# Layer 0's feed-forward, up half: seven block products for eight, weight sums made by accumulating DMAs, and adaLN units spread over single weight units

## The chip, the cores and the metric

One core of a Trainium2 chip runs the kernel. The metric is the device time in microseconds (us) of one execution. The engines named below are PE (TensorE, the matrix products), DVE (VectorE), ACT (ScalarE), POOL (GpSimd) and SP (SyncE, which here does nothing but issue DMAs; POOL issues some too). L97 is line 97 of the kernel's code.

## The reference

Two layers over 512 latent tokens ("x") and 256 context tokens ("c") of width 1024. Layer 0 mixes tokens by retention, layer 1 by differential attention; each layer ends with a gated feed-forward, and scales, shifts and gates of every sub-layer come from a conditioning vector (adaLN). The change is in the feed-forward of layer 0, where latent and context tokens go through the same weights:

```
def conv_ffn(u, w_up, conv_w, conv_b, w_down):
    val, gate = jnp.split(u @ w_up, 2, axis=-1)          # w_up: 1024 x 5632, hidden 2816 = 22 x 128
    return (jax.nn.silu(dwconv3(gate, conv_w, conv_b)) * val) @ w_down
...
    shm, scm, gm, shf, scf, gf = ada_mod(c, ada_w[l], ada_b[l])   # silu(c) @ ada_w + ada_b
    fx = conv_ffn(modulate(rms_norm(h_x, norm_g[l, 2]), shf, scf), ffn_w_up[l], ...)
    fc = conv_ffn(modulate(rms_norm(h_c, norm_g[l, 2]), cshf, cscf), ffn_w_up[l], ...)
```

Everything is float32.

## The kernel before

Every float32 product is made of three products of numbers of fewer bits: `split` writes an operand as H (a rounded copy, by ACT) and L (the rest, operand minus H, by DVE), and `mm3` (L96 to L99) issues H*H, H*L and L*H into the same PSUM bank. Weights come in units of 128 x 1024 (512 KB): SP loads one into `wraw` (three buffers, L64), ACT and DVE split it into `wH` and `wL` (L59, L60).

The stages follow one another: retention of layer 0 (four heads), its output product `ret_out` (`sublayer_out`, banks `pso`, first the latent tokens, then the context), the feed-forward's up half (banks `psf`), its down half (`sublayer_out` again, `pso`), then layer 1. No table sets the order. A scheduler places the instructions in the order of the code, weight loads and splits are pulled ahead by a priority, and a tile pool's number of buffers decides how far ahead a load can run.

The up half works on one block f of 128 hidden columns after another, 22 in all. For each f there are two units, gate and value (class `FFNUp`). Each is 8 row blocks of the weights (k) x 3 products, once over the 512 latent columns `ux` and once over the 256 context columns `uc`: 96 matmuls for one f, 48 of 512 columns and 48 of 256. `conv` then makes the hidden row block: ACT scales the gate (L322), two DVE operations add the neighbours (L323, L325), ACT applies SiLU (L327), and DVE multiplies by the value (L328) into `hTx` and `hTc`, which stay in SBUF until the down half splits them (`lxH`, `lxL`).

Between units `ada_next` computes adaLN values that later sub-layers need: an adaLN unit is one more 512 KB load through the same three `wraw` buffers and one or two DVE reductions (L164). Before the change 36 of the 80 stand in the retention (`ada_next(2)` or `(3)` after groups of weight units) and 44 in the up half, two for each f.

Just ahead of the up half the last steps of `ret_out` are: finish the latent tokens (`fin`, `sc`), transpose and modulate them into `ux` while PE does the context's output product, then the same for the context (`ctx_part`, L854 of the changed code), which runs while PE does the first products over x.

Of the kernel before, what the change touches and what calls it, by code (L numbers as in the profile page):

```python
# [9 lines left out]
F32 = mybir.dt.float32  # L10
# [20 lines left out]
def tile_hybrid_backbone(ctx: ExitStack, tc: tile.TileContext, A, out, dbg=None):  # L31
# [163 lines left out]
    class UT:  # L195
        def __init__(self):
            self.xH = [s2(F32R, name="uxH") for _ in range(KT)]
            self.xL = [s2(F32R, name="uxL") for _ in range(KT)]
            self.cH = self.cL = None

        def add_ctx(self):
            self.cH = [s2(F32R, (P, 2, 256), name="ucH") for _ in range(4)]
            self.cL = [s2(F32R, (P, 2, 256), name="ucL") for _ in range(4)]

        def part(self, p, k):

            if p == "c":
                return self.cH[k // 2][:, k % 2, :], self.cL[k // 2][:, k % 2, :]
            if isinstance(p, int) and p >= 4:
                o = slice((p - 4) * P, (p - 3) * P)  # L210
                return self.cH[k // 2][:, k % 2, o], self.cL[k // 2][:, k % 2, o]
            o = slice(p * P, (p + 1) * P) if isinstance(p, int) else {
                "x": slice(0, 512), "g0": slice(0, 256), "g1": slice(256, 512)}[p]
            return self.xH[k][:, o], self.xL[k][:, o]
# [146 lines left out]

    l0 = tc.tile_pool(name="l0", bufs=1)
# [32 lines left out]
    def ada_w(k):  # L395
        for kh in range(2):
            wada[k, kh] = W(A["ada0"][k * 2 + kh], late=k % 2 == 1, eng=nc.gpsimd if 2 * k + kh in (5, 9, 13, 4, 6, 0) else None, big=True)
# [69 lines left out]
    def first_ctx():  # L467
        U.add_ctx()
        norm_pair(psp, U, "c", xs[4:6], 0, 0)
# [8 lines left out]
    cb = l0p.tile([P, 2, 1024], F32, name="cb")  # L478
# [90 lines left out]
    for h in range(4):  # L569
# [3 lines left out]
        for qi in range(2):  # L573
            px = [bank("psqx") for _ in range(2)]
            pc = bank("psqc", (P, 2, 256))
            for c in range(2):
                w = qw.pop(0) if qw else W(win[w0 + 4 + 2 * qi + c])
                feat(U, w, px[c], "x")
                if h == 0 and qi == 0 and c == 0:
                    first_ctx()  # L580
                    qw.append(W(win[5]))
                    constants()
                    first_gate_ctx()
                feat(U, w, pc[:, c, :], "c")
# [18 lines left out]
            ada_next(2)  # L603
# [72 lines left out]
        ada_next(3)  # L676
# [25 lines left out]
        ada_next(2)  # L702
# [15 lines left out]
    def sublayer_out(nk, unit, lx, lc, chunk, prev, dst_x, dst_c, layer, sub_i, hook, pre):  # L718
# [8 lines left out]
        for k in range(nk - 2):  # L727
            w, lt = W(unit(k)), lx(k)
# [12 lines left out]
        def ahead(k):  # L741
            for j in range(min(k + 3, nk - 1) + 1):
                if j not in lcs:
                    lcs[j] = lc(j)
                if j == len(wcs) and j <= k + 2:
                    wcs.append(W(unit(j), "s6" if j % 2 == 0 else False))
# [5 lines left out]
        u = UT()  # L752
        side = []
# [13 lines left out]
        def keep(t):  # L767
# [3 lines left out]
                4: lambda: (keep(2), sc(2)), 5: lambda: (keep(3), sc(3), tr(0)), 8: lambda: tr(1)}  # L771
# [18 lines left out]
        def ctx_part():  # L790
# [3 lines left out]
            u.add_ctx()  # L794
            norm_pair(psp, u, "c", [xn[4], xn[5]], layer, sub_i)
# [3 lines left out]
    up0 = {}  # L799

    def pre_up():
        return [W(A["up"][0, i], True) for i in range(2)]

    u, ctx_part, first = sublayer_out(
        16, lambda k: A["ret_out"][k], lhs_x(load_y(0, 512)), lhs_c(load_y(512, 768)), 2, tok_src,
        lambda t: rows(h1d, t), lambda t: rows(h1d, t), 0, 1, lambda: y_out(3, prev_y), pre_up)
    flush_rows(psp)
    F = FFNUp(psp, u, 0, True, ada_next)
    F.w[0, 0], F.w[0, 1] = first
    F.run(0, 0, "x")  # L810
    F.run(0, 1, "x")
    ctx_part()
    F.run(1, 0, "x")
    F.conv(0, "x")
    F.run(0, 0, "c")
    F.run(0, 1, "c")
    F.run(1, 0, "c")
    F.conv(0, "c")
    for p in ("x", "c"):
        F.run(1, 1, p)  # L820
    F.conv(1, "x")
    F.conv(1, "c")
    F.rest(2)
# [3 lines left out]
    def pre_in():  # L827
# [3 lines left out]
        NF, lambda k: A["down"][0, k], lhs_x(lambda k: F.hx[k]), lhs_c(lambda k: F.hc[k]), 5, lambda t: rows(h1d, t),  # L831
        lambda t: rows(h2d, t), None, 1, 0, lambda: flush_rows(psp), pre_in)
# [10 lines left out]
    l0.__exit__(None, None, None)  # L843
# [477 lines left out]
    keep = [(k, W(A["down"][1, k], True), lx(k)) for k in range(NF - late, NF)]  # L1321
# [100 lines left out]
```

## Time and profile before

| | before |
|---|---|
| time, median of 3 runs | 2208.4 us (2206.65 to 2209.94) |
| the profiled execution's own time | 2208.85 us |
| its span in the trace | 2207.0 us |
| mean granted PE clock | 0.986 of full speed |
| busy share of the span: PE, DVE, ACT, POOL | 97%, 56%, 38%, 11% |
| up half of layer 0 on PE | 880.68 us to 1249.48 us |

The span is what the trace covers; the time lies 1.85 us above it. The busy shares are means over stages with different limits, so the rows further down take the stages apart by stretches of 40 us. The up half is found by the names of PE's banks: it begins with the first `psf` product and ends with the first `pso` product of the down half.

### The profile page before, as it was taken

To read this page: it belongs to the slowest core of one execution; us is meant where nothing else is said; L and a number is where in the kernel's file an instruction comes from. 1 tells how busy PE (TensorE), PEld (TensorE's weight loads), DVE (VectorE), ACT (ScalarE), POOL (GpSimd) and SP (SyncE) were. 2 spreads that over 40 slices of the span, in tenths; PEclk is the share of its full clock that TensorE was granted. 3 is DMA by queue.
4 is the path that set the end of the run, shared out by engine and by line. 5 is a ranking of instruction groups with operands and counts; after the bars stand their busy time and mean duration, and the time that the engine had idled before them with its cause. 6 is when DMAs were issued, how large, how long until landed. Compare 5 with 4: busy or idle time off the path is not lost. (4 is left out here: it accounts for less than half of the span.)

```text
span 2207.0 us, 28221 instructions
## 1 busy us (share of the span) xinstructions
PE 2150.1 (97%) x11136; PEld 1834.2 (83%) x11136; DVE 1227.3 (56%) x1928; ACT 849.1 (38%) x1494; POOL 243.1 (11%) x310
## 2 busy tenths in 40 slices
PE   7999999999999999999999999999999789999998
PEld 6888888888888888888888888888888678888887
DVE  6656553553553348665445625767797686444524
ACT  5432233332332346322222324654455465333412
POOL 3001101100200101000000001021232151000000
PEclk8999999999999999999999999999999899999999
DMA  7232322322223366434444435611111332333333
GB/s 261 87 111 86 129 78 69 118 92 69 101 86 110 113 212 205 141 117 140 125 128 126 151 105 194 207 51 46 44 44 32 112 122 101 102 97 99 109 97 124
DMA packets 82732, 250.68 MB, mean 114 GB/s; under 512 B 10104, under 2 KB 13480, under 8 KB 82472
## 3 DMA queue, kind: packets, MB, share of 16 engines
q1 hardware_dynamic: 79880, 241.00, 34.0%
q0 software_dynamic: 2720, 7.89, 0.9%
q8 instruction: 87, 1.43, 0.3%
q14 instruction: 45, 0.37, 0.1%
HBM read 232.05 MB, written 16.80 MB: 113 GB/s over the span
## 5 line engine op out<-in xcount | busy, mean ns | idle before, releaser
L60 DVE TENSOR_TENSOR wL<-wraw,wH 128x1024 fp32r<-128x1024 f32 x233 | 286.1, 1228 | 504.9 <-ACT wH L59 503.3
L59 ACT ACTIVATE wH<-wraw 128x1024 fp32r<-128x1024 f32 x259 | 273.9, 1058 | 642.9 <-PE psa L99 182.9
L97 PE MATMUL psf<-uxH,wH 128*128 128x512 f32 (+1 forms) x672 | 258.7, 385 | 0.0
L98 PE MATMUL psf<-uxL,wH 128*128 128x512 f32 (+1 forms) x672 | 258.5, 385 | 0.0
L99 PE MATMUL psf<-uxH,wL 128*128 128x512 f32 (+1 forms) x672 | 258.1, 384 | 0.1
L97 PE MATMUL pso<-wH,lxH 128*128 128x512 f32 x432 | 168.3, 390 | 0.6 <-ACT grow L183 0.3
L98 PE MATMUL pso<-wL,lxH 128*128 128x512 f32 x432 | 168.1, 389 | 0.0
L99 PE MATMUL pso<-wH,lxL 128*128 128x512 f32 x432 | 168.1, 389 | 0.0
L164 DVE CUSTOM_DVE_ANT_0 wraw<-wraw,cb 128x1024 f32<-128x1024 f32 x80 | 97.6, 1223 | 96.9 <-DMA wraw<-in_ada_rest_dram 96.3
L99 PEld LDWEIGHTS psf<-uxH,wL 128*128 128x128 f32 x672 | 126.3, 188 | 25.6 <-DVE wL L60 0.3
L97 PEld LDWEIGHTS psf<-uxH,wH 128*128 128x128 f32 x672 | 126.5, 188 | 23.9
L98 PEld LDWEIGHTS psf<-uxL,wH 128*128 128x128 f32 x672 | 126.5, 188 | 23.4
L97 PE MATMUL psa<-wH,uxH 128*128 128x512 f32 x352 | 137.0, 389 | 0.0
L98 PE MATMUL psa<-wL,uxH 128*128 128x512 f32 x352 | 137.0, 389 | 0.0
L99 PE MATMUL psa<-wH,uxL 128*128 128x512 f32 x352 | 136.9, 389 | 0.0
L137 POOL TENSOR_SCALAR st<-st 128x1 f32<-128x1 f32 x42 | 27.7, 658 | 675.4 <-ACT junk L136 673.9
L97 PEld LDWEIGHTS pso<-wH,lxH 128*128 128x128 f32 x432 | 81.1, 188 | 17.8 <-ACT grow L183 0.6
L99 PEld LDWEIGHTS pso<-wH,lxL 128*128 128x128 f32 x432 | 81.1, 188 | 17.0
L99 PE MATMUL psf<-ucH,wL 128*128 128x256 f32 x336 | 95.1, 283 | 0.0
L98 PE MATMUL psf<-ucL,wH 128*128 128x256 f32 x336 | 95.1, 283 | 0.0
L98 PEld LDWEIGHTS pso<-wL,lxH 128*128 128x128 f32 x432 | 81.1, 188 | 16.6
L97 PE MATMUL psf<-ucH,wH 128*128 128x256 f32 x336 | 94.9, 282 | 0.0
(360 smaller groups left out, 5104.9 us busy)
## 6 DMA issues: line engine op xcount, KB each, us to landing
wraw<-in_up_dram SPq DMA_DIRECT2D x88, 512.0 KB, 3.6
wraw<-in_ada_rest_dram SPq DMA_DIRECT2D x80, 512.0 KB, 3.7
wraw<-in_down_dram SPq DMA_DIRECT2D x66, 512.0 KB, 3.6
wraw<-in_ret_in_dram SPq DMA_DIRECT2D x64, 512.0 KB, 3.7
wraw<-in_ret_out_dram SPq DMA_DIRECT2D x32, 512.0 KB, 3.8
wraw<-in_diff_in_dram SPq DMA_DIRECT2D x24, 512.0 KB, 3.6
wraw<-in_ada_dram SPq DMA_DIRECT2D x16, 512.0 KB, 7.3
wraw<-in_diff_out_dram SPq DMA_DIRECT2D x16, 512.0 KB, 3.8
```

What stands on the lines that cost most here:

```text
L59: nc.scalar.activation(out=h, in_=x, func=AF.Copy)
L60: (eng or nc.vector).tensor_tensor(out=l, in0=x, in1=h.bitcast(F32), op=ALU.subtract)
L97: nc.tensor.matmul(ps, l[0], r[0], start=first, stop=False)
L98: nc.tensor.matmul(ps, l[0], r[1], start=False, stop=False)
L99: nc.tensor.matmul(ps, l[1], r[0], start=False, stop=last)
L137: nc.gpsimd.tensor_scalar(out=s[:, 2:3], in0=s[:, 0:1], scalar1=s[:, 1:2], scalar2=EPS, op0=ALU.add, op1=ALU.add)
L164: nc.vector.tensor_tensor_reduce(out=o, in0=raw, in1=cb[:, v, :], scale=1.0, scalar=0.0, op0=ALU.mult, op1=ALU.add, accum_out=adaF[:, laye ...
```

## The change

The up product of one f is seen as a 2 x 2 by 2 x 2 block product: the weights' rows in two halves and its two units (gate, value), the tokens in pairs of 128-column halves. Seven products of sums replace the eight (Winograd's form). Each of the seven (`product`) is 4 row blocks x 3 = 12 matmuls of 384 columns (256 of x, 128 of c), 84 for one f. What each part does:

- **Token sums.** `Seven.sums` makes four sums or differences and seven splits for the tokens, once, in `x_part` (four calls, inside the context half of `ret_out`) and `ctx_part`. They live in 14 tiles `tH`, `tL` of the pool `s6`, which grows from 8 to 16 buffers; `s2` shrinks from 48 to 31. So two `s6` buffers are left for what follows.
- **Weight sums.** `seven_w(f)` loads the unit g and three more tiles, `sa` (512 KB), `sb` (512 KB) and `v2` (256 KB). Four DMAs issued by POOL add to them in flight: 512 KB and 256 KB from DRAM, then two of 256 KB from `sa` into `sb`, which must wait for `sa`'s sum. `sa` and `sb` are `s6` tiles, so each has one buffer; for f=1 these buffers are first held by the two `ufc` tiles of `ctx_part`. The splits are one of 1024 columns and five of 512.
- **Combining.** Seven DVE additions of 384 columns (L935) and two ACT copies (`p1`, `p5`) put gate and value together; the convolution runs over all 768 columns at once from SBUF.
- **Hidden rows.** They go to DRAM (`hd`, 384 KB for each f, issued by POOL), and the down half loads them again (`yin`, issued by SP).
- **adaLN.** `ada_next(1)` after each single weight unit: 60 units stand in the retention, some 20 in the up half, one for each f.

```diff
     def s2(dt=F32, shape=(P, 512), name="s2"):
-        return sp.tile(list(shape), dt, tag="s2", name=name, bufs=48)
+        return sp.tile(list(shape), dt, tag="s2", name=name, bufs=31)
     def s6(dt=F32, shape=(P, 1536), name="s6"):
-        return sp.tile(list(shape), dt, tag="s6", name=name, bufs=8)
+        return sp.tile(list(shape), dt, tag="s6", name=name, bufs=16)
...
                     mm3(pss[i], u.part(t, k), w(kk * 512, 512), k == 0, k == KT - 1)
+            ada_next(1)
...
-        ada_next(3)
...
+    ORDER = (1, 6, 5, 7, 2, 3, 4)
+    class Seven:
...
+                    self.H[i], self.L[i] = s6(F32R, (P, 4, 384), name="tH"), s6(F32R, (P, 4, 384), name="tL")
+        def sums(self, lo1, hi1, lo2, hi2, T, at):
+            a, b, c, d = T
+            stt = nc.vector.scalar_tensor_tensor
+            sub(a, lo1, hi1)
+            sub(b, hi2, hi1)
+            stt(out=c, in0=hi2, scalar=-1.0, in1=a, op0=ALU.mult, op1=ALU.subtract)
+            stt(out=d, in0=c, scalar=-1.0, in1=lo2, op0=ALU.mult, op1=ALU.subtract)
+            for i, x in ((1, lo1), (6, c), (5, a), (7, b), (2, lo2), (3, hi2), (4, d)):
+                split(at(self.H[i]), at(self.L[i]), x)
...
+        def ctx_part(self, xn):
+            uf = [s6(shape=(P, 4, 256), name="ufc") for _ in range(2)]
...
+    def seven_w(f):
+        up = A["up"][0]
+        g = load_raw(up[2 * f])
+        sa, sb = s6(name="sa")[:, :1024], s6(name="sb")[:, :1024]
+        v2 = s2(name="v2")
+        nc.sync.dma_start(out=sa.rearrange("p (u c) -> p u c", u=2),
+                          in_=up[2 * f : 2 * f + 2, :, :512].rearrange("u p c -> p u c"))
+        nc.sync.dma_start(out=sb, in_=up[2 * f])
+        nc.sync.dma_start(out=v2, in_=up[2 * f + 1, :, 512:])
+        with tc.high_priority(offset=AHEAD):
+            acc = lambda o, x: nc.gpsimd.dma_start(out=o, in_=x, accum_op=ALU.add)
+            acc(sa, up[2 * f + 1])
+            acc(sb[:, 512:], up[2 * f, :, :512])
+            for i in range(2):
+                acc(sb[:, i * 512 : i * 512 + 512], sa[:, 512:])
...
+            split(H, L, g)
+            ops[1], ops[2] = (H[:, :512], L[:, :512]), (H[:, 512:], L[:, 512:])
+            for i, x in ((6, sb[:, :512]), (5, sa[:, 512:]), (7, sa[:, :512]), (3, sb[:, 512:]), (4, v2)):
+                H, L = s2(F32R, name="opH"), s2(F32R, name="opL")
+                split(H, L, x)
+                ops[i] = H, L
+        return ops
+    def ffn0(u, ops, ctx_part, then):
...
+                for k in range(4):
+                    s = slice(k * P, k * P + P)
+                    mm3(banks[i][:, o], (H[:, s], L[:, s]), u.at(i, k, p), k == 0 and p != "c", k == 3 and p != "x")
...
+            if f == 0:
+                for i in ORDER[:4]:
+                    product(i, "x")
+                ctx_part()
+                for i in ORDER[:4]:
+                    product(i, "c")
...
+                if i == 1:
+                    nxt.append(seven_w(f + 1) if f + 1 < NF else then())
...
+            nc.vector.scalar_tensor_tensor(out=v, in0=v, scalar=-1.0, in1=c, op0=ALU.mult, op1=ALU.mult)
+            nc.gpsimd.dma_start(out=hd[f], in_=v)
+            ada_next(1)
+            ops = nxt[0]
```

How the instructions stand on three engines follows; names carry a number for each tile.

On POOL, in the second half of the up half (blocks f=12 and f=13 of the changed kernel; `sa` and `sb` are the weight sums of one f, `val` is the hidden row block of the f two earlier):

```order
L888 DMA sa_9200<-in_up_dram 128x1024
L888 DMA sb_9201<-in_up_dram 128x512
L970 DMA hd_5965<-val_9127 128x768
L888 DMA sb_9201<-sa_9200 128x512 x2
L888 DMA sa_9357<-in_up_dram 128x1024
L888 DMA sb_9358<-in_up_dram 128x512
L970 DMA hd_5965<-val_9282 128x768
L888 DMA sb_9358<-sa_9357 128x512 x2
```

Before, POOL has no row of its own there. The rows nearest to that place are the last norms and gate rows ahead of the up half, and then a table of layer 1:

```order
L137 TENSOR_SCALAR st_7203<-st_7203 128x1
L184 DMA gd_100<-grow_7216 8x128
L138 TENSOR_TENSOR st_7203<-st_7203,mhalf_78 128x1
L184 DMA gd_100<-grow_7221 8x128
L849 DMA dcos_11756<-in_rope1_dram 128x512
```

So POOL now issues four sums and a store for each f, and the store of the hidden rows of two blocks earlier stands ahead of the last two sums (`sb` from `sa`).

On DVE, most of a turn of the changed kernel in the same stretch, from the last operation on the hidden rows of f=11 to the additions for f=12 (`L60` are the L halves of splits, `L935` the combining additions):

```order
L969 SCALAR_TENSOR_TENSOR val_9282<-val_9282,conv3_9328 128x768
L60 TENSOR_TENSOR wL_9523<-wraw_9510,wH_9522 128x1024
L60 TENSOR_TENSOR opL_9372<-sb_9358,opH_9371 128x512
L60 TENSOR_TENSOR opL_9376<-sa_9357,opH_9375 128x512
L60 TENSOR_TENSOR opL_9380<-sa_9357,opH_9379 128x512
L60 TENSOR_TENSOR opL_9384<-sb_9358,opH_9383 128x512
L60 TENSOR_TENSOR opL_9388<-v2_9359,opH_9387 128x512
L935 TENSOR_TENSOR u2_9406<-psf_9393,p1_9391 128x384
L935 TENSOR_TENSOR gate3_9455<-psf_9442,p1_9391 128x3x128
L935 TENSOR_TENSOR u4_9422<-u2_9406,p5_9421 128x384
L935 TENSOR_TENSOR u3_9438<-psf_9425,u2_9406 128x384
L935 TENSOR_TENSOR gate3_9455<-psf_9457,u4_9422 128x3x128
```

and before, for one f, with two adaLN units of two vectors in it:

```order
L164 ISA wraw_8259,adaF_90<-wraw_8259,cb_798 128x1024
L164 ISA adaF_90 128x1
L60 TENSOR_TENSOR wL_8206<-wraw_8203,wH_8205 128x1024
L323 SCALAR_TENSOR_TENSOR conv_8197<-psf_8098,cw_89,conv_8197 128x255
L325 SCALAR_TENSOR_TENSOR conv_8197<-psf_8098,cw_89,conv_8197 128x255
L164 ISA adaj_8322,adaF_90<-wraw_8320,cb_798 128x1024
L164 ISA adaF_90 128x1
L328 TENSOR_TENSOR hTx_8189<-psf_8134,conv_8190 128x512
L164 ISA wraw_8320,adaF_90<-wraw_8320,cb_798 128x1024
L164 ISA adaF_90 128x1
L171 TENSOR_TENSOR adaF_90<-adaF_90,adab_87 128x8
L328 TENSOR_TENSOR hTc_8196<-psf_8159,conv_8197 128x256
```

Behind the L half of the unit g stand the five L halves of f=13 that read `sb`, `sa` and `v2`, and only then the additions that empty the banks of f=12.

On SP, one f of the changed kernel:

```order
L64 DMA wraw_10424<-in_ada_rest_dram 128x1024
L64 DMA wraw_10440<-in_up_dram 128x1024
L883 DMA sa_10442<-in_up_dram 128x2x512
L885 DMA sb_10443<-in_up_dram 128x1024
L886 DMA v2_10444<-in_up_dram 128x512
```

and before, where adaLN units and weight units take turns:

```order
L64 DMA wraw_8528<-in_ada_rest_dram 128x1024
L64 DMA wraw_8531<-in_up_dram 128x1024
L64 DMA wraw_8587<-in_ada_rest_dram 128x1024
L64 DMA wraw_8603<-in_up_dram 128x1024
```

Where there were two adaLN units and two weight units for one f, there are now one adaLN unit and four weight loads.

## Rows read from the trace of the kernel before

**Rows 1.** The page: busy time of each engine, and SP's queue (packets, MB, share).

```profile
PE 2150.1 (97%) x11136; PEld 1834.2 (83%) x11136; DVE 1227.3 (56%) x1928; ACT 849.1 (38%) x1494; POOL 243.1 (11%) x310
...
q1 hardware_dynamic: 79880, 241.00, 34.0%
```

**Rows 2.** Stretches of 40 us: PE, PEld, DVE, ACT, POOL busy, PEclk, DMA share, GB/s.

```profile
820.00:860.00 40.00, 40.00 (x194) 33.40 (x192) 33.02 (x59) 28.01 (x68) 9.46 (x16) 1.00 0.65 214
860.00:900.00 40.00, 39.12 (x185) 32.27 (x185) 29.78 (x51) 25.08 (x56) 6.07 (x10) 1.00 0.61 207
...
1020.00:1060.00 40.00, 40.00 (x235) 35.48 (x234) 18.86 (x30) 9.50 (x14) 0.00 (x0) 1.00 0.41 130
```

**Rows 3.** Timeline of PE, up half: start us, us, line, operation.

```profile
880.68 0.47 PE L97 MATMUL psf<-uxH,wlH 128*128 128x512 f32 x1
...
891.68 1.91 PE L242 MATMUL pst<-ident,xn 128*128 128x128 f32 x16
...
898.91 0.28 PE L97 MATMUL psf<-ucH,wlH 128*128 128x256 f32 x1
...
1229.93 0.28 PE L97 MATMUL psf<-ucH,wH 128*128 128x256 f32 x1
...
1232.80 0.40 PE L97 MATMUL psf<-uxH,wH 128*128 128x512 f32 x1
...
1238.27 0.28 PE L97 MATMUL psf<-ucH,wH 128*128 128x256 f32 x1
...
1249.48 0.40 PE L97 MATMUL pso<-wH,lxH 128*128 128x512 f32 x1
```

**Rows 4.** DVE by line and shape, 900 to 1250 us: busy, mean ns | idle before.

```profile
L164 DVE CUSTOM_DVE_ANT_0 wraw<-wraw,cb 128x1024 f32<-128x1024 f32 x44 | 53.8, 1224 | 96.4 <-DMA wraw<-in_ada_rest_dram 96.3
L60 DVE TENSOR_TENSOR wL<-wraw,wH 128x1024 fp32r<-128x1024 f32 x41 | 50.1, 1221 | 24.3 <-ACT wH L59 24.3
L325 DVE SCALAR_TENSOR_TENSOR conv<-psf,cw,conv 128x511 f32<-128x511 f32 x21 | 15.8, 750 | 0.6
...
L328 DVE TENSOR_TENSOR hTx<-psf,conv 128x512 f32<-128x512 f32 x21 | 14.4, 685 | 2.7 <-PE psf L99 2.0 <-ACT conv L327 0.8
L325 DVE SCALAR_TENSOR_TENSOR conv<-psf,cw,conv 128x255 f32<-128x255 f32 x22 | 10.6, 483 | 0.8
...
L328 DVE TENSOR_TENSOR hTc<-psf,conv 128x256 f32<-128x256 f32 x21 | 8.8, 420 | 0.1
L60 DVE TENSOR_TENSOR lxL<-hTx,lxH 128x512 fp32r<-128x512 f32 x10 | 6.4, 689 | 0.0
```

**Rows 5.** ACT by line and shape, same stretch and columns.

```profile
L59 ACT ACTIVATE wH<-wraw 128x1024 fp32r<-128x1024 f32 x41 | 43.2, 1054 | 55.7 <-PE psf L98 52.8 <-PE psf L99 2.8
...
L59 ACT ACTIVATE lxH<-hTx 128x512 fp32r<-128x512 f32 x12 | 6.5, 617 | 0.0
```

**Rows 6.** DMA issues of the whole span: KB each, median us from issue to landing.

```profile
wraw<-in_up_dram SPq DMA_DIRECT2D x88, 512.0 KB, 3.6
...
wraw<-in_ada_dram SPq DMA_DIRECT2D x16, 512.0 KB, 7.3
...
yTd<-yo POOLq DMA_DIRECT2D x16, 256.0 KB, 4.1
...
yd<-yT POOLq DMA_DIRECT2D x4, 256.0 KB, 2.4
...
dsin<-in_rope_dram POOLq DMA_DIRECT2D x1, 256.0 KB, 5.9
```

**Rows 7.** Timeline: a buffer freed by DVE, SP's next load; POOL issuing four stores.

```profile
1009.74 0.08 DVE L164 DVE_READ_ACCUMULATOR2_ANT adaF<- 128x1 f32 x1
...
1009.86 0.33 SPq L64 DMA_DIRECT2D wraw<-in_up_dram  x1
...
234.32 2.39 POOL L559 DMA_DIRECT2D yTd<-yo  x4 [8.40 <-ACT yo L557]
```

**Rows 8.** Timeline of DVE ahead of the context's transposes.

```profile
888.33 0.88 DVE L220 TENSOR_SCALAR xn<-hn,st 128x512 f32<-128x512 f32 x2 [1.03 <-POOL st L138]
```

More of the change, by code (lines that the diff above doesn't have):

```diff
@@ L196, in __init__, with slot @@
         def __init__(self):
[L197 to L203, printed above, removed]
-        def part(self, p, k):
[L207 to L211, printed above, removed]
+            self.t = {}
+        def slot(self, j):
+            if j // 3 not in self.t:
+                self.t[j // 3] = s6(F32R, (P, 3, 512), name="u")
+            return self.t[j // 3][:, j % 3, :]
+        def part(self, p, k):
+            if p == "c" or isinstance(p, int) and p >= 4:
+                a, n = (0, 256) if p == "c" else ((p - 4) * P, P)
+                o = slice((k % 2) * 256 + a, (k % 2) * 256 + a + n)
+                return self.slot(16 + k // 2)[:, o], self.slot(20 + k // 2)[:, o]
             o = slice(p * P, (p + 1) * P) if isinstance(p, int) else {
                 "x": slice(0, 512), "g0": slice(0, 256), "g1": slice(256, 512)}[p]
-            return self.xH[k][:, o], self.xL[k][:, o]
+            return self.slot(k)[:, o], self.slot(8 + k)[:, o]
     def scaled(hs, inplace=False):
@@ L396, in ada_w @@
         for kh in range(2):
-            wada[k, kh] = W(A["ada0"][k * 2 + kh], late=k % 2 == 1, eng=nc.gpsimd if 2 * k + kh in (5, 9, 13, 4, 6, 0) else None, big=True)
+            wada[k, kh] = W(A["ada0"][k * 2 + kh], late=("s6" if kh == 0 else True) if k % 2 == 1 else False, eng=nc.gpsimd if 2 * k + kh in (5, 9, 13, 4, 6, 0) else None, big=True)
     def scale_in(hs):
@@ L467, in first_ctx @@
     def first_ctx():
-        U.add_ctx()
         norm_pair(psp, U, "c", xs[4:6], 0, 0)
@@ L727, in sublayer_out @@
         for k in range(nk - 2):
-            w, lt = W(unit(k)), lx(k)
+            w, lt = begun[k] if k < len(begun) else (W(unit(k)), lx(k))
             for t in range(4):
@@ L745, in ahead @@
                 if j == len(wcs) and j <= k + 2:
-                    wcs.append(W(unit(j), "s6" if j % 2 == 0 else False))
+                    wcs.append(W(unit(j), j % 3 == 2 if seven else "s6" if j % 2 == 0 else False))
         ahead(0)
@@ L751, in sublayer_out @@
                 run(t, k, w, lt)
-        u = UT()
-        side = []
+        u = Seven() if seven else UT()
         hs, xn = {}, {}
@@ L770, in sublayer_out @@
         side = {0: lambda: fin(2), 1: lambda: fin(3), 2: lambda: (keep(0), sc(0)), 3: lambda: (keep(1), sc(1)),
-                4: lambda: (keep(2), sc(2)), 5: lambda: (keep(3), sc(3), tr(0)), 8: lambda: tr(1)}
+                4: lambda: (keep(2), sc(2)), 5: lambda: (keep(3), sc(3))}
+        if seven:
+            side |= {6 + 2 * q: lambda q=q: u.x_part(q, xn) for q in range(4)}
+        else:
+            side[5] = lambda: (keep(3), sc(3), tr(0))
+            side[8] = lambda: tr(1)
         for t in (4, 5):
@@ new lines, in modulated_on @@
+    def modulated_on(uf, ps, k, v, act):
+        a, b = adaF[:, 0, v, 4, k : k + 1], adaF[:, 0, v, 3, k : k + 1]
+        if act:
+            nc.scalar.activation(out=uf, in_=ps, func=AF.Identity, scale=a, bias=b)
+        else:
+            nc.vector.tensor_scalar(out=uf, in0=ps, scalar1=a, scalar2=b, op0=ALU.mult, op1=ALU.add)
+    hd = dr.tile([NF, P, 768], F32, name="hd")
+    nop = [0]
+    def seven_w(f):
[11 more added lines that the diff above has]
+            acc(sb[:, 512:], up[2 * f, :, :512])
+            for i in range(2):
+                acc(sb[:, i * 512 : i * 512 + 512], sa[:, 512:])
+            ops = {}
+            H, L = wp.tile([P, 1024], F32R, tag="wH", name="wH", bufs=2), wp.tile([P, 1024], F32R, tag="wL", name="wL", bufs=2)
+            split(H, L, g)
[5 more added lines that the diff above has]
+        return ops
@@ L809, in tile_hybrid_backbone @@
[L809 to L823, printed above, removed]
+    l0.__exit__(None, None, None)
+    down, hx = lambda k: A["down"][0, k], lhs_x(load_y(hd, 0, 512))
+    begun = ffn0(u, first, ctx_part, lambda: [(W(down(0)), hx(0)), (W(down(1), True), hx(1))])
@@ L1320, in tile_hybrid_backbone @@
     hp = {t: load_h(rows(h3d, t)) for t in range(4)}
-    keep = [(k, W(A["down"][1, k], True), lx(k)) for k in range(NF - late, NF)]
+    keep = [(k, W(A["down"][1, k], "s6"), lx(k)) for k in range(NF - late, NF)]
     for t in (2, 0, 1, 3):
```

132 lines of the change are left out of this document (109 added, 23 removed).

## Prediction

> **What bounds the kernel now.** I read the page first: PE is busy 97% of the span, DVE 56% [rows 1]. So time goes only where PE gets less work or is made to wait. Then the stretches of 40 us: in the up half PE is busy all 40.00 us at a granted clock of 1.00, while DVE has 18.86 us of work and the DMA engines 0.41 of their time [rows 2]. PE's timeline says what the half is made of. It runs from 880.68 to 1249.48 us. Inside it 24 matmuls of 256 columns take 1232.80 - 1229.93 = 2.87 us (0.120 each) and the next 24 of 512 columns 5.47 us (0.228 each) [rows 3]. One f is two of each: 16.68 us, and 22 of them, 367 us, with 1.9 us of transposes, fill the half. The reader is to see a stage bound by PE alone, with little else to do on DVE and in DMA. The change takes from PE and gives to both.
>
> **What PE gains.** A matmul of 384 columns isn't in the trace. Between 0.120 and 0.228 the straight line gives 0.174. 84 of them are 14.6 us for one f, 2.1 less than now, and 46 us over 22. It is had only if the weights of the next f come every 14.6 us and the first ones come in time.
>
> **What the weights of one f now pass through.** `sa` has one buffer, and so has `sb`. The chain from one use to the next is:
> - three L halves on DVE that free `sa` (operands 6, 5, 7): 3 x 0.689 = 2.1 us [rows 4];
> - SP's load of `sa`, 512 KB: 3.6 us [rows 6];
> - POOL's sum of 512 KB into `sa`. The trace has no sum by DMA. The nearest rows are loads of 512 KB at 3.6 us and, for the sixteen units of `in_ada`, 7.3 us [rows 6]; below a plain load it can't well be. SP's queue moved 241 MB in 34.0% of 2207 us [rows 1], so at full rate 321 GB/s. Of the 3.6 us then 1.6 are bytes. A sum must also read what it adds to. If that doubles the bytes, it is 5.2 us; I take 5.3;
> - POOL's sum of 256 KB from `sa` into `sb`, which can't start before the one above has landed. POOL's DMAs of 256 KB land in 2.4 to 5.9 us, most in 4.1 [rows 6]. I take 4.1, the row with the most DMAs (16);
> - ACT's H half of operand 6: 0.6 us [rows 5];
> - four hand-overs, each about 0.1 us (a reader's end at 1009.82, SP's issue at 1009.86) [rows 7]: 0.4.
>
> Together 16.1 us, between 12.7 and 19.9 with the ends of the two unknown prices. That is above PE's 14.6.
>
> A second chain holds from f=12 on, where the store of older hidden rows stands ahead of the `sb` sums on POOL. DVE ends a block (768 columns, by the step from 256 to 512 columns 0.95 us), POOL issues the store (2.39 / 4 = 0.6 [rows 7]), then the sum runs (4.1), then the H half (0.6), and DVE waits in front of operand 6 all the while, with the additions of the block before queued behind it. After the wait DVE has five L halves (3.4), seven additions of 384 columns (0.55 each between 0.420 and 0.685: 3.9), four convolution steps (2 x 0.75 + 2 x 0.48 = 2.5) and an adaLN reduction of 1.2 before the next block's end [rows 4]. With the hand-overs this is 17.7 us if nothing overlaps; part of it may (the reduction needs nothing of this block), so I take 16.7. The additions that stand behind operand 6 also free banks: product 5 of a block needs the bank that `u2` of the block before empties, some 4 us after the wait ends, and PE has only product 6 (2.1 us) to fill that. PE stands about 1.8 us, which the longer turn covers except in the last f.
>
> So I take 16.1 us for the first half and 16.7 for the second, on average **16.4 us for one f**, against 16.68 before and 14.6 by PE.
>
> **The start.** Without any wait product 6 of f=1 would start at 880.7 + 1.9 + 14.6 + 2.1 = 899 us. Two things are late.
> - The context. Before, the norm of the context ended at 889.2 us [rows 8] and PE took the transposes at 891.68, when its products over x, 18.2 us in all before the first context product at 898.91, still ran [rows 3]. Now the cover is four products of x, 48 matmuls of 256 columns, 5.8 us. DVE has 33 and 30 us of work in the two stretches there [rows 2]; the change adds some 12 us to these 63 of 80 (four times eleven operations of 256 columns and a modulation, less sixteen splits and eight modulations of 256; the halves of f=0), with waits for norms in between, so it is nearly full: I take 3 us late, and some 2 more where L halves stand ahead of the context's norm. Transposes then end at 896.1. `ctx_part` on DVE is four modulations (1.7) and the unit of f=1 (1.2), and eight operations of 512 columns until the last reader of `ufc` (5.5): 904.5.
> - The weights of f=1. `sa` and `sb` take the two buffers that `ufc` held until then. From 904.5 the load, both sums, the splits and the hand-overs are 3.6 + 5.3 + 4.1 + 0.6 + 0.7 + 0.4 = 14.7 us: 919.2. PE itself would be there at about 916 (context products 2, products 2, 3, 4 and 1 at 2.1 us each, after operand 6 of the context at 905.9).
>
> So the start costs 20 us, with bounds of 6 and 33.
>
> **The sum.** Product 6 of f=1 at 919.2, 20 turns of 16.4 (328), then six products and the bank wait (14.3): the half ends at 1261.5 instead of 1249.48, **+12.0 us**. Against the profiled execution's 2208.85 us that is 2220.9; the median of the runs shown is 0.45 lower, and I say 2221.
>
> **Costed at nothing.** 24 more adaLN units in the retention are 24 to 48 reductions of 1.2 us on DVE over some 640 us; DVE's mean share there is far from full [rows 1], and PE hides them. If a split stands behind them where PE waits it may cost up to 5 us. The hidden rows' way through DRAM is 8.6 MB written and read again; the loads run two row blocks ahead in the down half, beside its own 512 KB units. Fewer `s2` buffers may shorten that; bound 0 to 5 us. Both fewer adaLN units and no `hTx` buffers help nothing that PE waits for.
>
> **Rivals.**
> 1. *The sums are quick and PE keeps the pace: faster.* If both sums together take 7.9 us or less (3.6 + 4.1, a plain load and a plain store), the chain is at most 14.6 and PE sets the turn. Product 6 of f=1 then starts at 917, and the half ends at 917 + 20 x 14.57 + 12.5 = 1221: -28.5 us, **2180**. With a turn of 15.2 it is 2194; were the start not late at all, 2162. For it: DMA has room (0.41), and one row of POOL's DMAs is 2.4. Against it: the other rows are 4.1 and 5.9 and none of them adds. The Trainium skill (DMA: Bandwidth & Descriptors, "Anatomy of one DMA — SWDGE (gpsimd) path") gives POOL's DMAs as 2.0 us plus bytes at 436 GB/s: an estimate of 3.2 and 2.6 us, with which this rival would hold. By that rule a 256 KB DMA of POOL would land in 2.6, where 16 of them here took 4.1.
> 2. *Sums at half rate, DMA engines full: much slower.* For one f there are 2304 KB of loads, 1280 KB of sums and 384 KB of stores, 4.06 MB, 12.7 us at 321 GB/s; with the sums' destinations read as well 5.37 MB, 16.7 us. Then each DMA waits for others, and the two sums go to their upper ends, 7.3 and 5.9. Turns of 18 to 21 us end the half at 1296 to 1356: **2256 to 2315**. For it: one group of 512 KB loads took 7.3 us. Against it: DMA's share is 0.41 now with 2 MB for one f. The Trainium skill (Collectives: The Full Stack, "The bandwidth ceiling: the fold count and why AG ≠ RS ≠ AR") says that an addition in the DMA engines needs two source reads and so moves at half the rate of a copy. No row here shows an addition.
> 3. *It comes out even.* Gain and start cancel at a turn of 15.8 us.
>
> **How the numbers follow.** About 0.2% (4.4 us) is what a measurement of this kernel can tell from no change: turns above 16.0 us are slower, below 15.6 faster. My forecast (16.0 to 17.6) has 0.45, rival 1 0.33, rival 2 0.11, even 0.11. Slower is 0.45 + 0.11 = 0.56. The range must reach into both rivals: from 2182, near the end that PE sets, to 2262, a turn of 18.4. The likeliest case alone gives 2213 to 2245.
>
> **What would show it.** In the profile after: twelve matmuls of 384 columns in 2.1 us; PE idle in the up half, ahead of product 6, put down to the H or L half of operand 6 and behind it to a DMA into `sb`; POOL's 512 KB sums landing in 4.7 to 6 us and the 256 KB ones in 3.5 to 5; product 6 of f=1 near 919 us; some 16.4 us from one f to the next. I am wrong if PE is busy throughout the half (rival 1), if the DMA share is above 0.9 (rival 2), or if time is lost in the retention or the down half.

## The result and the profile after

The changed kernel takes 2275.7 us, the median of 4 runs (2274.95 to 2277.75), against 2208.9 of the kernel before beside it: a ratio of 1.0308, with a 95% interval of 1.0296 to 1.0321. It is slower, as forecast, but by 67 us and not by 12.

The page's first rows and its DMA queues, to be held against [rows 1]:

```profile
span 2273.0 us, 28672 instructions
...
PE 2141.7 (94%) x10920; PEld 1859.6 (82%) x10920; DVE 1344.2 (59%) x2172; ACT 901.8 (40%) x1585; POOL 329.5 (14%) x419
...
q1 hardware_dynamic: 95368, 266.96, 35.5%
q0 software_dynamic: 17152, 45.39, 9.0%
```

The loss sits in one place. On PE's timeline the first `psf` product starts at 883.77 us and the down half's first `pso` product at 1316.46: the up half takes 432.7 us, where it took 368.8 [rows 3]. The span grew by 66.0; 63.9 of them are here, 3.1 ahead of it, and the rest of the kernel is 1.0 us shorter.

Three stretches of the changed kernel (columns as in [rows 2]): the start of the half, and two of its middle.

```profile
880.00:920.00 40.00, 26.20 (x135) 23.86 (x134) 25.30 (x46) 16.37 (x37) 10.83 (x15) 0.76 0.63 162
...
1000.00:1040.00 40.00, 34.73 (x182) 33.77 (x181) 27.28 (x46) 15.99 (x27) 8.05 (x10) 0.91 0.82 218
...
1160.00:1200.00 40.00, 34.81 (x191) 34.18 (x190) 25.66 (x43) 13.57 (x22) 8.67 (x11) 0.96 0.85 221
```

PE is no longer full, and DVE, with 25 to 27 us, is no bound either. What has doubled is the DMA share: 0.41 before, 0.77 to 0.86 in the seven stretches of 40 us from 960 to 1240 us. From one block to the next POOL issues its first sum every 18.7 us (930.76 for f=2, 1285.65 for f=21: 354.9 / 19). PE is busy 363.2 us of the half, where 22 blocks at 14.56 and the transposes would be 322: behind the waits its granted clock is lower, 0.91 as the mean of the half. The chain that follows has no link on PE, so it is not this that sets the turn.

One whole turn, from the timeline of all engines (start us, us, engine, line, operation, and in brackets the idle time before it and what ended it). `opH` and `opL` are the halves of the summed weights:

```profile
999.58 0.69 DVE L60 TENSOR_TENSOR opL<-sb,opH 128x512 fp32r<-128x512 f32 x1 [6.34 <-ACT opH L59]
1000.19 1.29 DVE L60 TENSOR_TENSOR opL<-sa,opH 128x512 fp32r<-128x512 f32 x2
...
1001.51 0.38 SPq L883 DMA_DIRECT2D sa<-in_up_dram  x1
...
1002.11 0.33 SPq L885 DMA_DIRECT2D sb<-in_up_dram  x1
...
1002.49 0.42 SPq L886 DMA_DIRECT2D v<-in_up_dram  x1
...
1002.50 0.47 ACT L939 ACTIVATE p<-psf 128x384 f32<-128x384 f32 x1
...
1002.96 0.42 SPq L64 DMA_DIRECT2D wraw<-in_ada_rest_dram  x1
...
1003.02 0.44 PE L97 MATMUL psf<-tH,opH 128*128 128x384 f32 x1 [1.27 <-ACT p L939]
...
1003.43 0.43 SPq L64 DMA_DIRECT2D wraw<-in_up_dram  x1
...
1005.90 0.86 POOL L888 DMA_DIRECT2D sa<-in_up_dram  x1 [7.46 <-DVE u L935]
...
1013.78 0.87 POOL L888 DMA_DIRECT2D sb<-sa  x1 [5.75 <-DMA sa<-in_up_dram]
...
1017.11 0.63 ACT L59 ACTIVATE opH<-sb 128x512 fp32r<-128x512 f32 x1 [6.55 <-DMA sb<-sa]
...
1017.78 0.69 DVE L60 TENSOR_TENSOR opL<-sb,opH 128x512 fp32r<-128x512 f32 x1 [5.86 <-ACT opH L59]
```

This is the forecast chain, link by link. DVE frees `sa` at 1001.48 and SP loads it at once (1.9 us after the turn's start). POOL's 512 KB sum goes out at 1005.90 (4.4 later: 3.7 for the load, and 0.7 until POOL issues), and the sum of 256 KB from `sa` can go only at 1013.78 (7.9). The H half follows at 1017.11 (3.3) and the L half at 1017.78 (0.7): 18.2 us. PE's own wait ends with `p`, the copy that empties product 1's bank; that copy stands on ACT behind the H halves, and these wait for the sum. So a row that names `p` at L939 is still the sum's wait.

What the DMAs of the half cost (columns as in [rows 6], 940 to 1300 us):

```profile
sb<-sa POOLq DMA_DIRECT2D x40, 256.0 KB, 3.4
sa<-in_up_dram SPq DMA_DIRECT2D x19, 512.0 KB, 3.7
...
sa<-in_up_dram POOLq DMA_DIRECT2D x19, 512.0 KB, 7.6
```

Why 7.6 to 7.9 us is seen in stretches of 2 us of the turn above. A packet is counted in the stretch in which it begins, with all its time, so that a short stretch can show a share above 1:

```profile
1004.00:1006.00 2.00, 2.00 (x13) 2.00 (x13) 2.00 (x5) 0.00 (x0) 0.10 (x1) 1.00 1.04 410
...
1008.00:1010.00 2.00, 2.00 (x13) 2.00 (x13) 1.81 (x5) 0.28 (x1) 0.03 (x1) 1.00 1.11 309
1010.00:1012.00 2.00, 2.00 (x14) 2.00 (x13) 1.91 (x3) 0.56 (x1) 0.00 (x0) 1.00 0.99 201
1012.00:1014.00 2.00, 2.00 (x13) 2.00 (x12) 0.00 (x0) 0.00 (x0) 0.22 (x1) 1.00 0.98 180
```

The DMA engines are full (share about 1.0) from 1004 to 1014 us, first at 410 GB/s, when they serve the loads of `sb`, `v2`, the adaLN unit and the next g that SP issued in one go behind `sa`, and at the end at 180 GB/s, when the two sums from DRAM are left (the 256 KB one into `sb` goes out at 1007.15 and lands after 7.5 us). The mean share of 0.82 hides this: the burst lies just where the chain runs through. Behind it the share falls to 0.47 (1014 to 1016 us), while the chain waits for the sum from `sa`: so the engines have room left in the turn, and it is the chain that uses it up.

### The profile page after: what moved, and what is told of

The parts are those of the page before. It is cut to its first block, busy times and chain, and to the rows that moved or that the text cites. A ratio compares the mean times of both kernels' runs of the same rounds, so it can differ in the third digit from the quotient of the medians.

```text
span 2273.0 us, 28672 instructions
## 1 busy us (share of the span) xinstructions
PE 2141.7 (94%) x10920; PEld 1859.6 (82%) x10920; DVE 1344.2 (59%) x2172; ACT 901.8 (40%) x1585; POOL 329.5 (14%) x419
## 5 line engine op out<-in xcount | busy, mean ns | idle before, releaser
L60 DVE TENSOR_TENSOR wL<-wraw,wH 128x1024 fp32r<-128x1024 f32 x215 | 263.9, 1228 | 403.3 <-ACT wH L59 401.1
L97 PE MATMUL psf<-tH,opH 128*128 128x384 f32 (+2 forms) x452 | 165.3, 366 | 61.8 <-ACT p L939 55.7
L97 PE MATMUL psa<-wH,u 128*128 128x512 f32 x528 | 205.5, 389 | 0.0
L98 PE MATMUL psa<-wL,u 128*128 128x512 f32 x528 | 205.5, 389 | 0.0
L99 PE MATMUL psa<-wH,u 128*128 128x512 f32 x528 | 205.4, 389 | 0.0
L98 PE MATMUL psf<-tL,opH 128*128 128x384 f32 (+2 forms) x452 | 162.0, 358 | 2.5 <-DVE tL L60 2.5
L99 PE MATMUL psf<-tH,opL 128*128 128x384 f32 (+2 forms) x452 | 162.5, 359 | 0.0
L97 PEld LDWEIGHTS psf<-tH,opH 128*128 128x128 f32 x452 | 95.9, 212 | 68.9 <-ACT p L939 62.4
L99 PE MATMUL psf<-u,wL 128*128 128x512 f32 (+1 forms) x336 | 127.4, 379 | 0.1
L97 PE MATMUL psf<-u,wH 128*128 128x512 f32 (+1 forms) x336 | 127.3, 379 | 0.0
L98 PE MATMUL psf<-u,wH 128*128 128x512 f32 (+1 forms) x336 | 127.3, 379 | 0.0
L99 PEld LDWEIGHTS psa<-wH,u 128*128 128x128 f32 x528 | 99.1, 188 | 20.7
L97 PEld LDWEIGHTS psa<-wH,u 128*128 128x128 f32 x528 | 99.2, 188 | 20.4
L98 PEld LDWEIGHTS psa<-wL,u 128*128 128x128 f32 x528 | 99.1, 188 | 20.2
L60 DVE TENSOR_TENSOR opL<-sb,opH 128x512 fp32r<-128x512 f32 x44 | 30.3, 688 | 114.7 <-ACT opH L59 114.7
```

The lines of the kernel that those rows point to most:

```text
L60: (eng or nc.vector).tensor_tensor(out=l, in0=x, in1=h.bitcast(F32), op=ALU.subtract)
L97: nc.tensor.matmul(ps, l[0], r[0], start=first, stop=False)
L98: nc.tensor.matmul(ps, l[0], r[1], start=False, stop=False)
L99: nc.tensor.matmul(ps, l[1], r[0], start=False, stop=last)
```

## The experiments

The half's length is given from the first `psf` to the first `pso` product, as above (432.7 us in the changed kernel). A turn is the usual distance between DVE's last operations on two blocks. The times of single runs are single executions.

**The additions left out.** The sums are plain copies, so what they should add is missing.

```diff
-            acc = lambda o, x: nc.gpsimd.dma_start(out=o, in_=x, accum_op=ALU.add)
+            acc = lambda o, x: nc.gpsimd.dma_start(out=o, in_=x)
```

> The four sums of one f are issued as plain copies of the same bytes to the same places, in the same order and with the same waits; the additions are left out. Theory A (one buffer for sa and one for sb make load, sum of sa, sum of sb and splits one chain; a sum takes about twice the DMA time of a copy): the 512 KB step lands in 4 to 5 us instead of 7.7, the 256 KB step in about 3, a turn is 15 to 16 us instead of 18.7, the time 2195 to 2225. Rival B (the price is POOL's issuing and its waits, not the addition): landings and turn stay within 1 us, 2260 to 2276. Rival C (DVE's or PE's own work sets the turn): no change, 2276.

2226.9 us, the half 378.0, a turn of 16.1; the time is just past theory A's upper end. The 512 KB step landed in 6.2 us and the 256 KB step in 2.7. So the addition counts, but a copy in this place is no 4 us either: the forecast of 4 to 5 missed. It is 2.4 us above the same load by POOL with nothing beside it (3.8, in the tail further down); what differs here is the DMAs in flight beside it.

What the additions cost the DMA engines stands in the rows of POOL's queue, 940 to 1200 us (packets, MB, share), first of the changed kernel, then of the copies, with the copies' landing:

```profile
q0 software_dynamic: 9054, 23.63, 44.4%
...
q0 software_dynamic: 7512, 27.66, 27.1%
...
sa<-in_up_dram POOLq DMA_DIRECT2D x16, 512.0 KB, 6.2
```

At full rate that is 205 GB/s with the additions and 393 without, with the stores of the hidden rows in both: bytes that are added take the engines about twice the time of bytes that are copied.

**No adaLN loads in the up half.**

```diff
-            ada_next(1)
+            ada_next(2 if n < 3 else 1)
```

> The 20 adaLN units of the up half stand in the retention instead (two after each of three weight units in four, where one stood). That takes one 512 KB load for each f out of the up half. Theory A in its strict form (the sum of sa takes 7.7 us by itself): a turn stays 18.7, about 2276. Theory A with contention (the sums share the DMA engines with the loads issued just before them): the sum of sa lands about 1.5 us earlier, a turn is 17.1, about 2243. Rival C (DVE's work): 1.2 us less on DVE for each f, a turn 17.5.

2256.1 us. The half fell to 398.0 and the turn to 16.7, below the 17.1 that contention was to give; the sum landed in 5.9 us. The strict form, in which the sum is 7.7 by itself, is out. But the half starts at 902.76, 19.0 us later: 80 units in the retention are too many there, while the change's 60 cost it 3.1. The cover that I counted on does end, between the two.

**The last two sums on DVE.**

```diff
-                acc(sb[:, i * 512 : i * 512 + 512], sa[:, 512:])
+                o = sb[:, i * 512 : i * 512 + 512]
+                nc.vector.tensor_tensor(out=o, in0=o, in1=sa[:, 512:], op=ALU.add)
```

> The last two of the four sums (sb from sa) are additions on DVE instead of DMAs. Theory A: the chain loses a DMA of 3.4 us and gains one addition of 0.7, and 512 KB of sums no longer share the engines: a turn of 15.5 to 16.2, 2213 to 2227. Rival C (DVE's work sets the turn): 1.4 us more on DVE for each f, a turn of 20, 2300.

2238.5 us, the half 389.3, a turn of 16.5. The link of 3.4 us is gone, and so is most of that time; DVE, with more work, was not the bound. The turn is 0.3 us above the upper end of the forecast, and the time 11.5 us above it.

**All sums by POOL's additions in SBUF**, from the two units alone, with two buffers for the second one.

```diff
+        b = s6(name="b")
+        nc.sync.dma_start(out=b[:, :1024], in_=up[2 * f + 1])
...
+            for o, x, y in ((b12, b1, b2), (b1, b1, g1), (g1, g1, b12), (g2, g2, g1)):
+                nc.gpsimd.tensor_tensor(out=o, in0=x, in1=y, op=ALU.add)
```

> No accumulating DMA at all: only the two units of f are loaded, and POOL makes the four sums from them in SBUF with additions of 512 columns; the second unit has two buffers. Theory A: the chain is gone, PE sets the turn at 14.6 to 15.2, the start is some 5 us shorter, 2180 to 2200. Rival C (DVE, POOL and the combining set the turn): POOL needs 4 times about 1.4 us and can't slow the turn by itself, so DVE's 12 us or waits between the engines would: 17 to 19 us a turn, 2240 to 2280.

2237.0 us (2232.9 to 2239.1), a ratio of 1.0132 (1.0115 to 1.0149) to the kernel before; the half 381.9. My expectation was wrong: without any sum by DMA the turn is still 16.4. DVE's groups by shape, 940 to 1200 us (columns as in [rows 4]), and then POOL's, show slower operations:

```profile
L60 DVE TENSOR_TENSOR wL<-wraw,wH 128x1024 fp32r<-128x1024 f32 x16 | 31.0, 1935 | 0.0
...
L959 DVE SCALAR_TENSOR_TENSOR conv<-gate,cw,conv 128x511 f32<-128x511 f32 x15 | 19.7, 1314 | 7.6 <-ACT conv L957 7.6
```

```profile
L891 POOL TENSOR_TENSOR b<-b,wraw 128x512 f32<-128x512 f32 x16 | 30.8, 1923 | 1.3
L891 POOL TENSOR_TENSOR wraw<-wraw,b 128x512 f32<-128x512 f32 x16 | 23.7, 1479 | 25.5 <-DVE wL L60 25.5
L891 POOL TENSOR_TENSOR b<-b 128x512 f32<-128x512 f32 x16 | 20.5, 1281 | 25.0 <-DMA b<-in_up_dram 25.0
```

The same L half takes 1935 ns where it took 1221 [rows 4], and a convolution step 1314 for 750, while POOL's additions take 1281 to 1923. These are means of two kinds. Of the L halves ten ran beside an addition of POOL for more than half their time and took 2304 ns, and five beside none took 1216; POOL's addition `b<-b`, beside next to nothing on DVE, took 1281. An addition of DVE that reads a bank (`gate` from `psf` and `u`) took 546 beside POOL and is not slowed. So where both work on SBUF the two engines slow each other.

That this alone makes the turn is not shown. DVE also waits, 2.5 us in each turn, and mostly for the load of the adaLN unit, with the L half of g and additions that empty PE's banks behind it:

```profile
L164 DVE CUSTOM_DVE_ANT_0 wraw<-wraw,cb 128x1024 f32<-128x1024 f32 x16 | 23.8, 1487 | 40.1 <-DMA wraw<-in_ada_rest_dram 40.1
```

**The same with a fourth load buffer.** `s2` has 29 buffers for 31 here, as in every later kernel with four.

```diff
-        raw = s6(name="wraw")[:, :1024] if big else wp.tile([P, 1024], F32, tag="wraw", name="wraw", bufs=3)
+        raw = s6(name="wraw")[:, :1024] if big else wp.tile([P, 1024], F32, tag="wraw", name="wraw", bufs=4)
```

> POOL's additions with a fourth wraw buffer. In the run with three, SP's load of the next unit waited for the adaLN unit's buffer, and POOL's adds behind it. Theory D (the load buffers are the second chain): a turn falls from 16.5 to 15 or less, 2195 to 2208. Rival E (DVE's order: additions that free PE's banks stand behind splits that wait for POOL, and POOL and DVE slow each other's operations): the turn stays within 0.4 us of 16.5, 2230 to 2240.

2231.8 us, a turn of 16.5, and PE waits for DVE's additions: the three load buffers were not what bound that version. What PE waited for and what SP waited for, 940 to 1200 us (us in total, times, longest):

```profile
PE psf L97 <- DVE u L930: 17.6, 13, 1.5
...
SPq L882 <- DVE opL L60: 242.7, 16, 15.7
```

SP's loads of a turn, the adaLN unit's among them, go out only when an L half lets go of a buffer of `b`. So a loop is left from DVE's L halves over SP's loads to DVE's wait for the adaLN unit, and slowed operations stand in it; no run takes the two apart.

**Two buffers for `sa`, and the sums of `sb` in g's own buffer**, all sums by DMA, four `wraw` buffers, the split of g ahead of the sums; and the same with an idle tile (`pad`, the second kernel alone) that puts `sa` back into one buffer.

```diff
-        sa, sb = s6(name="sa")[:, :1024], s6(name="sb")[:, :1024]
+        sa, sb = s6(name="sa")[:, :1024], g
...
-        nc.sync.dma_start(out=sb, in_=up[2 * f])
...
+        pad = s6(name="pad")
+        nc.gpsimd.memset(pad[:, :1], 0.0)
```

> The accumulating DMAs stay. The sums that went into sb are made in the load buffer of the unit g itself once g is split (so the second load of g, 512 KB for each f, is gone), which leaves sa both spare buffers; wraw has four buffers for three. Theory A (load, sum and sum of one f can't start before the f ahead has let go of its one buffer): the chain of f+1 now runs beside that of f, a turn is set by what comes next, the DMA engines (some 13 to 14 us of work for each f) or the waits between DVE and PE that the runs without the chain showed: 15.5 to 16.5 us, 2205 to 2228. Rival B (a turn is the time that the DMA engines need for its bytes at the share of 0.85 that they reach): 18.7 less 1.6, 17.1, 2241.

> The same kernel with a tile that holds nothing taken between two sa, so that sa is back in one buffer and all else is the same (POOL writes one column of that tile, some 0.3 us). Theory A: the turn is 1 to 2 us longer than with two buffers, 17 to 18 us, 2238 to 2260. Rival B (bytes alone): no difference between the two.

2295.6 and 2303.8 us, turns of 20: slower than the changed kernel, with 512 KB less to load for each f. Both theories are contradicted, and the timeline of POOL in the first of the two says by what:

```profile
1047.00 0.86 POOL L887 DMA_DIRECT2D wraw<-in_up_dram  x1 [8.50 <-DVE wL L60]
...
1047.63 1.12 POOL L887 DMA_DIRECT2D wraw<-sa  x1
...
1048.32 1.33 POOL L887 DMA_DIRECT2D sa<-in_up_dram  x1
...
1051.30 0.85 POOL L887 DMA_DIRECT2D wraw<-sa  x1 [1.66 <-DMA wraw<-in_up_dram]
```

The sum into g's buffer must wait for the L half of g (`wL`), which stands late in DVE's order; POOL's queue keeps the sums behind it, and then the next block's 512 KB sum goes out ahead of the last one of this block. These two land after 10.7 and 9.5 us. The pair doesn't tell whether the buffer counts: in both the chain runs through POOL's queue.

**That, with the last two sums on DVE**, and of it one with `sa` in one buffer, one with three `wraw` buffers (and 31 of `s2`), and a second run, beside one in which the first block's loads and sums start three steps earlier (the edit below is that one's alone).

```diff
-            if k == nk - 1:
+            if k == nk - (4 if seven else 1):
```

> Two buffers for sa, g's own buffer for the sums, four wraw buffers, and the last two sums on DVE: 768 KB of sums by DMA for each f, 1.4 us more on DVE (some 13.5 us of 14.6). Theory A: neither chain nor DMA engines bind, 14.8 to 15.6 a turn, 2190 to 2208. Rival E: as DVE is fuller and stands ahead of the banks, 16 to 16.5, 2217 to 2230.

> The kernel of the last run (last two sums on DVE, g's buffer for the other, four wraw buffers) with a tile that holds nothing between two sa, so that sa has one buffer and all else is as there. Theory A (the one buffer makes the chain): PE, busy without a gap with two buffers, waits again; a turn goes from 14.6 to 15.5 or more, 2212 or above. If the buffer is not what counts, it stays within 3 us of 2196.

> The same kernel with two sa buffers and three wraw buffers for four. Theory D (the load buffers are a second chain, as the unit g now keeps its buffer until its sums are split): a turn of 15.5 to 16.5, 2212 to 2235. If sa's buffers alone count: 2196.

> The kernel with the last sums on DVE, two sa buffers and four wraw buffers, timed against the kernel before: one look gave 2196, so a ratio of 0.993 to 0.996 if that holds.

> The same kernel, and the loads and sums of the first block are issued three steps of the context's output product earlier. In the run before, PE stood 3.2 us in front of product 6 of f=0 and 5.6 us later for the context, and its granted clock was down to 0.50 in the stretch 910 to 920. If the first sums are what is late: 3 to 6 us less, 2190 to 2193. If the context's norm and the token sums on DVE are: within 1 us of the run before.

The first run gave 2196.0 us and a half of 346.1; on PE's timeline no wait is left behind the start. Run again it took 2197.9 us as the median of 10, but from 2188.7 to 2214.7, a ratio of 0.9970 (0.9944 to 0.9995). One buffer for `sa` gave 2212.0, three for `wraw` 2213.1, with halves of 360.4 and 361.9 and six waits of PE in each behind the start, of 0.5 to 3.8 us, all but one in the second part of the half. These are single executions inside the spread of the kernel that they were to differ from, so they lean towards the buffers but settle nothing. The earlier start gave 2199.0 (2188.6 to 2215.8), the same; its half is 3 us shorter and starts 4 us later. Nor does all of the difference between runs lie in the half: what follows it took 957.5 us before and 956.5 in the changed kernel, but 960.0 to 968.7 in the profiled executions of the two versions with POOL's sums and of these five runs, for a reason that no run shows.

**The disputed price by itself.** Behind the changed kernel's last store, where nothing else is left to do, loads and sums one after the other, and then sums beside three loads each.

```diff
+            for _ in range(5):
+                go(t)
...
+            for i in range(3):
+                nc.sync.dma_start(out=comp[i], in_=src)
+            nc.gpsimd.dma_start(out=t, in_=src, accum_op=ALU.add)
```

> The changed kernel with a tail behind its last store, where no other work is left: five loads of 512 KB by SP, five by POOL, five sums of 512 KB from DRAM, five of 256 KB from DRAM, five of 256 KB from SBUF, one after the other, and then four sums of 512 KB, each issued with three loads of 512 KB by SP. The tail makes the time longer; only its landings are read. Theory A1 (the addition itself is slow): a sum of 512 KB lands in 5.5 us or more alone, against 3.6 for a load. Theory A2 (the company of loads makes it slow): alone it lands within 1 us of a load by POOL, and beside three loads in 7 us or more. Both may hold: then about 5 alone and 7 to 8 beside loads.

DMA issues of the tail, 2255 to 2440 us (columns as in [rows 6]):

```profile
beside<-in_up_dram SPq DMA_DIRECT2D x12, 512.0 KB, 4.6
loadSP<-in_up_dram SPq DMA_DIRECT2D x5, 512.0 KB, 3.6
loadPOOL<-in_up_dram POOLq DMA_DIRECT2D x5, 512.0 KB, 3.8
sumDRAM<-in_up_dram POOLq DMA_DIRECT2D x5, 512.0 KB, 5.4
...
sumBESIDE<-in_up_dram POOLq DMA_DIRECT2D x4, 512.0 KB, 9.6
halfDRAM<-in_up_dram POOLq DMA_DIRECT2D x5, 256.0 KB, 4.2
halfSBUF<-halfDRAM POOLq DMA_DIRECT2D x5, 256.0 KB, 3.3
```

Both hold. Alone the sum is 5.4 us, 1.6 above POOL's plain load. Beside three loads it is 9.6. The 4.6 of the loads is a median over three unlike places; those of the first round one by one (issued at 2391.41, 2391.84 and 2392.31 us, the sum at 2391.93) are:

```profile
beside<-in_up_dram SPq DMA_DIRECT2D x1, 512.0 KB, 3.7
beside<-in_up_dram SPq DMA_DIRECT2D x1, 512.0 KB, 4.7
beside<-in_up_dram SPq DMA_DIRECT2D x1, 512.0 KB, 9.1
```

The first two land ahead of the sum and lose little. The third, issued 0.4 us behind the sum, loses 5.5 us and lands together with it: both pay for the company.

**One sum left to DMA.** The kernel with the earlier start (two `sa` buffers, the sums in g's own buffer, four `wraw` buffers, the last two sums on DVE), and the 256 KB sum from DRAM made by POOL in SBUF.

```diff
-            acc(sb[:, 512:], up[2 * f, :, :512])
+            nc.gpsimd.tensor_tensor(out=sb[:, 512:], in0=sb[:, 512:], in1=sb[:, :512], op=ALU.add)
```

> The kernel with the earlier start, and the 256 KB sum from DRAM made by POOL in SBUF instead: of the four sums one is left to DMA. Theory A: 256 KB less of sums, so PE keeps its pace in all executions and the spread of 27 us between them shrinks; 2185 to 2198. Rival E (a POOL addition slows DVE's operations beside it, as in the runs with all sums on POOL, and PE waits for DVE): 2200 to 2215.

2190.6 us (2188.7 to 2191.6), a ratio of 0.9923 (0.9904 to 0.9942): 0.8% faster than the kernel before, less than 2% but clear of 1, and 85 us faster than the changed kernel; the four executions lie within 3 us, where ten with the earlier start alone spread over 27. Two stretches of its middle:

```profile
1040.00:1080.00 40.00, 40.00 (x233) 40.00 (x232) 36.91 (x66) 18.30 (x29) 9.75 (x9) 1.00 0.67 196
1120.00:1160.00 40.00, 40.00 (x233) 40.00 (x232) 35.38 (x61) 17.29 (x27) 10.76 (x9) 1.00 0.63 187
```

PE is busy 40.00 of 40 us at a granted clock of 1.00, and the turn is 14.56 us, PE's own pace. Its 512 KB sum still lands in 9.1 us; with two `sa` buffers and no second sum by DMA behind it, PE does not wait for that. Rival E did not come: POOL's one addition takes 2146 ns on average, but DVE's operations keep their times (the L half of g 1225), so here POOL alone pays. The half is 343.4 us in the profiled execution, against 343.1 with the earlier start alone. What differs between these two executions is the part behind the half, 958.6 us for 965.3.

## Why the prediction was wrong

**What bounds the kernel, and what PE gains:** right. 84 matmuls of 384 columns take 14.56 us where PE doesn't wait; I had 14.6.

**The chain of one f:** the place, the order of its links and the wait that it makes are as told. What failed is one term, "POOL's sum of 512 KB into `sa`", taken at 5.3 us. That is right for the sum alone (5.4), and wrong where it stands: 7.6 to 7.9, past the upper end of 7.3. I priced it as one DMA with nothing beside it, although SP's order in the same text shows it issued right behind five loads. Held together, the runs give its parts: a load by POOL 3.8; 2.4 more for the company (a copy there took 6.2); 1.5 more for the addition. The last two are not clean parts, since the run with copies also made the 256 KB sum beside it a copy. The other links moved less: the `sb` sum 3.3 for 4.1, POOL's issue 0.6 later, the L halves 1.9 for 2.1. 16.1 becomes 18.2 in the turn shown, and 18.7 on average.

**The second chain, from f=12:** did not bind. The turns there are no longer than before it (18.6 us on average for 18.8), since the sum that the hidden rows' store stands ahead of waits for `sa` longer than for the store, as POOL's timeline shows:

```profile
1144.20 0.58 POOL L970 DMA_DIRECT2D hd<-val  x1 [3.60 <-DVE val L969]
1146.25 0.85 POOL L888 DMA_DIRECT2D sb<-sa  x1 [1.48 <-DMA sa<-in_up_dram]
```

**The start:** operand 6 of f=1 was split at 924.59 for 919.2 forecast, 5 us late. That block's 512 KB sum went out 3 us later than in my working (the half itself began 3.1 later), and landed after 9.0 us for 5.3, of which the `sb` sum gave back some.

**The sum:** of the 54 us that are missing between +12 and the span's +66, 46 are 20 turns at 18.7 for 16.4, 5 the start and 4 the last block; what follows the half gives 1 back.

**Costed at nothing:** right within its bounds for this change (3.1 us ahead of the half, -1.0 behind it; how much of the 3.1 is the adaLN units' and how much the token sums', no run tells), and near its end: 20 units more cost 19 us.

**The rivals:** rival 2 had the mechanism in part and the time: full DMA engines and sums at about half rate, 2256 to 2315. I gave it 0.11 and set a DMA share above 0.9 as its mark. The mean is 0.77 to 0.86; the burst that counts is at 1.0. I argued against it with the share of the kernel before (0.41 with 2 MB for one f), where the same working would have given twice the bytes and more, most of them issued within 2 us. The Trainium skill (Collectives: The Full Stack, "The bandwidth ceiling: the fold count and why AG ≠ RS ≠ AR") has the addition of a ring collective at half the rate of its copy, as it needs two source reads; a ring is not this case, but the ratio agrees with POOL's queue here, 205 GB/s with the additions and 393 without. The Trainium skill (DMA: Bandwidth & Descriptors, "Issuing engines are not separate DMA queues") says that all DMAs share the same engines and interleave, whoever issues them; that a sum took 9.6 us beside three loads against 5.4 alone, and that the third load ended with it, agrees.

Rival 1's end, PE's pace, was reached once the sums no longer held PE up: 2190.6 where it said 2180. Of the 10 us between, 6 lie ahead of the half, which starts at 887.03 us for 880.68 before, 3 in it and 1 behind it.

**What stays open:** how much of the last version's gain over the changed kernel is due to the second `sa` buffer, to the other buffers, to the load of g that fell away and to the fewer sums, since the runs that were to tell lie inside a spread of 26 us; why the executions of the version with two DMA sums spread so far; and what makes the part behind the half longer in some versions.

## What to carry to other kernels

A DMA on a chain is priced by what is in flight beside it, not by its landing with nothing beside it: look at which loads the issuing order puts in the same few microseconds, and at the DMA share there, not at its mean over a stage. A sum by DMA costs more than the load that it replaces, and what is in flight with it waits too, so it suits data that nobody waits for. And where a chain is cut, look at once for the next bound: with all sums on POOL it lay 2 us above PE's pace.

## What the runs showed that was not expected

- Beside three loads of 512 KB a sum of the same size took 4.2 us longer than alone, and the load issued just behind it 5.5 longer, while the two issued ahead of it lost 0.1 and 1.1.
- POOL's additions of 512 columns and DVE's operations on SBUF slow each other: an L half 1216 to 2304 ns, while an addition of DVE that reads a PSUM bank kept its 546.
- After PE's waits at the start of the changed kernel's half its granted clock was 0.50 (the level of 1.2 GHz) while it worked 8.89 of 10 us, and was near full again (0.94) in the next stretch:

```profile
905.00:910.00 5.00, 1.92 (x12) 1.59 (x12) 5.00 (x10) 3.02 (x6) 0.00 (x0) 0.76 0.38 100
910.00:920.00 10.00, 8.89 (x39) 8.89 (x40) 2.89 (x5) 0.51 (x1) 1.81 (x2) 0.50 0.95 248
920.00:930.00 10.00, 9.51 (x51) 9.19 (x51) 4.58 (x7) 4.53 (x8) 1.72 (x2) 0.94 0.60 142
```
